# The ConvFFN of a diffusion block on one core: another order of the down-projection's K chunks, and four smaller moves in its schedule

## Chip, core and metric

One Trainium2 chip, one core of it. The metric is device time in microseconds (us) of one execution. The kernel before takes 1344.51 us (median of three runs, 1343.38 to 1346.95).

## What is computed

One layer of a hybrid backbone over 1024 latent tokens of width 1024: a mixing sub-layer (windowed attention beside Fourier mixing), then a gated MLP with a convolution over the tokens. The change lies in the second one:

```python
def conv_ffn(h, w_up, conv_w, conv_b, w_down):
    u, gate = jnp.split(h @ w_up, 2, axis=-1)                 # 1024 x 2816 each
    up = jnp.pad(u, ((0, 0), (1, 1), (0, 0)))
    u = up[:, :-2] * conv_w[0] + up[:, 1:-1] * conv_w[1] + up[:, 2:] * conv_w[2] + conv_b
    return (jax.nn.silu(u) * gate) @ w_down                   # 1024 x 1024
x = x + gt2 * rmsnorm(conv_ffn(h2, ...), g_post2)
```

All of it is float32.

## The kernel before

**Products.** Every large matrix product is cut into 2 x 2 blocks, and each block product is formed by a Winograd variant of Strassen's scheme with seven products, P1 to P7. It works on sums and differences of the operands' blocks: S1 to S4 of one operand (made per pair in `do_add`, L245), T1, T2, T3 and T4n of the other. A float32 operand is split into a high and a low float32r part (`split`, L79: ScalarE copies the high part, VectorE subtracts it to get the low one), and a product of two tiles takes three matmuls (`mm3`, L83).

**Items.** One of the seven products of one *pair* of blocks is an *item*. The list `items` (`wino_items`, L201) is the order of TensorE's work in the MLP: 17 items that are written out by hand (`START`, L1885), then seven per pair, P1 P2 P4 P3 P6 P5 P7, where P4 and P3 belong to the pair before. Items are counted here from 0. There are 22 *up pairs* (one per tile of 128 hidden columns, in the order 0, 11, 1, 12, ... 10, 21); up pair i, from the fourth on (i = 3), begins at item 19 + 7(i - 3), and an up item has 12 matmuls. The 16 *down pairs* begin at item 152: four chunks of K tiles, `CH` (L1663), each with four pairs of token tiles. HF is 11; the chunks are the K tiles 0-1, 2-4, 5-7 and 8-10, in this order, so a down item has 6 matmuls in chunk 0 and 9 in the others. The last item is 265.

**What sets the order.** The whole MLP is under a manual schedule: each engine and each DMA queue does its work in the order in which the program emits it, and all loads and stores are issued by the SyncE queue (SP). `run2` (L352) goes through the items. For item k it emits, in this order: hooks placed with `at(k, ...)`; `ahead(k)` (L328), which fetches and prepares operands of the next items; `flush(k)`, what earlier steps left due at k; the item's matmuls; and after P1, P6 and P7 a ScalarE copy of the accumulator X (tile `snP`). What comes due later is evacuation: the one of P7 reads accumulator Y at k + 2 (`add(gt[1], pst, sn)`, L1734, tile `gg`, or `yd` in the down stage), and P3 of the same pair, two items after that, accumulates into the same Y, so P3 waits for this read. In the same way P4 waits for the copy of X after P7.

**Up stage.** `ahead` loads the weights 11 items ahead, and makes S1 and S3 five items ahead; S2 and S4 follow. The engine for these four sums is `seng[0]`: VectorE until L2102 sets it to GpSimd, just before the general loop starts at item 14, and VectorE again from item 131 (L1909). After an up pair's last product comes the convolution: ScalarE scales, VectorE does two scalar_tensor_tensor (L1710, L1711), ScalarE the SiLU, VectorE two gate products. The result g is the down stage's first operand and goes to HBM (`g_d`, L1669). For P1, P2 and P4 it is always split first (`g_ready`, L1678: a ScalarE cast, a VectorE subtraction, tiles `gh` and `gl`, and three items later two stores). For the sums of P3, P5, P6 and P7 (`g_sums`, L1684, four operations on GpSimd up to f = 19 and on VectorE after), `split_early` (L1666) says whether they are split there as well, two stores each, or stored as they are:

```python
def split_early(c, p):
    return p in ("P1", "P2", "P4") or c in (0, len(CH) - 1)
```

**Weights of the down stage.** `d_diffs(r, i)` (L1757), for K tile r: at item i four loads of `w_down` into four buffers (`wB`, 4 buffers in all), at i + 4 to i + 7 one VectorE subtraction each, at i + 6 to i + 9 one store each. Before, i is 16 + 12 r. `d_prep` (L1789) loads a chunk's rows again (`wdB`, `wdT`), one per item, and splits them (`dB`, `dT`).

**Down stage.** `do_fetch` (L222) loads an item's g: six items ahead in two DMAs where it was split, nine items ahead in one where it was not. In chunk 0 the two parts share one tile (`b...`, L231), 128 x 256 each. In the last chunk `finish` (L1846) follows each complete half row of the output:

```python
rs = rstd_steps(ssd[:, i, :], f"d{i}")
return [(1, rs[0]), (2, lambda: [rs[1](), d_out(i, 0, rs[2]), d_out(i, 1, rs[2])] and None),
        (4, lambda: [d_store(i, h) for h in range(2)] and None)]
```

`rs[0]` is two small VectorE operations and ScalarE's square root (L142 to L144), `rs[1]` four small VectorE operations; before them stand the squares (`d_square`, ScalarE, L1824) and the gate (`d_gate`). What belongs to the last pair (token tiles 3 and 7) is written out after the loop (L2106 to L2130).

Of the kernel before, what the change touches and what calls it, by code (L numbers as in the profile page):

```python
# [16 lines left out]
P = 128  # L17
# [3 lines left out]
NT = S // P  # L21
# [3 lines left out]
NF = FF // P  # L25
# [15 lines left out]
def block_kernel(ctx: ExitStack, tc: tile.TileContext, t: dict, out: bass.AP, dbg: dict):  # L41
# [15 lines left out]
    def dscr(name, shape, dtype=F):  # L57
        return dram.tile(shape, dtype, tag=name, name=name)
# [78 lines left out]
    def rstd_steps(parts, name):  # L137

        v, sq, r, n1, r2 = (tiny(f"{n}{name}", 1, 16) for n in ("v", "sq", "r", "n1", "r2"))

        def one():
            add(v, parts[:, 0:1], parts[:, 1:2])  # L142
            nc.vector.tensor_scalar(out=v, in0=v, scalar1=1.0 / D, scalar2=EPS, op0=ALU.mult, op1=ALU.add)
            nc.scalar.activation(out=sq, in_=v, func=AF.Sqrt)  # L144

        def two():
            nc.vector.reciprocal(out=r, in_=sq)
            nc.vector.scalar_tensor_tensor(out=n1, in0=r, scalar=v, in1=r, op0=ALU.mult, op1=ALU.mult)
            nc.vector.tensor_scalar(out=n1, in0=n1, scalar1=-0.5, scalar2=1.5, op0=ALU.mult, op1=ALU.add)
            mul(r2, r, n1)  # L150

        return one, two, r2

    def transpose8(xn, psf, name):

# [55 lines left out]
    def wino(pairs, items, psf, hooks, slots=False, seng=None):  # L211
# [10 lines left out]
        def do_fetch(j, p):  # L222
            ld, _, nm, _, nk = pairs[j]
            parts = ld[p]
            w = nk * P
            if len(parts) == 1:
                st[j][STA[p]] = s(f"r{p}_{nm}")[:, :w]
                load(out=st[j][STA[p]], in_=parts[0])
                return
            if 2 * w <= 512:  # L230
                both = s(f"b{p}_{nm}", R)  # L231
                st[j][p] = both[:, :w], both[:, w:2 * w]
            else:
                st[j][p] = s(f"h{p}_{nm}", R)[:, :w], s(f"l{p}_{nm}", R)[:, :w]
            for x, src in zip(st[j][p], parts):
                load(out=fbits(x), in_=src)
# [1423 lines left out]


    HF = NF // 2
    CH = [(0, HF % 3)] + [(c, 3) for c in range(HF % 3, HF, 3)]  # L1663
    place = {c0 + k: (c, k) for c, (c0, nk) in enumerate(CH) for k in range(nk)}

    def split_early(c, p):  # L1666
        return p in ("P1", "P2", "P4") or c in (0, len(CH) - 1)

    g_d = {(c, p): [dscr(f"g_d{c}{p}{i}", [NT // 2, P, nk * P]) for i in range(2 if split_early(c, p) else 1)]  # L1669
           for c, (_, nk) in enumerate(CH) for p in STA}  # L1670
    kept = {}

    def g_store(f, p, *parts):
# [10 lines left out]
    def g_sums(f):  # L1684

        (a11, a21), (a12, a22) = kept[f - HF], kept[f]
        s1 = s(f"gs{f}")

        early = split_early(place[f % HF][0], "P5")

        def step(p, op, d, a, b):
            return lambda: (op(d, a, b, nc.gpsimd if f < NF - 2 else None), [(2, lambda: g_ready(f, p, d)) if early else (2, lambda: g_store(f, p, d))])[1]

        return [(0, step("P5", add, s1, a21, a22)), (0, step("P7", sub, a21, a11, a21)),
                (1, step("P6", sub, a11, s1, a11)), (3, step("P3", sub, a12, a12, a11))]
# [143 lines left out]

    def down_pair(c, m):  # L1840
        last = c == len(CH) - 1
        ld = {p: [d[m] for d in g_d[c, p]] for p in STA}

        half = set()

        def finish(i, n):  # L1846

            first = i not in half
            half.add(i)
            if not first and m == NT // 2 - 1:  # L1850
                return None

            def squares():
                d_square(i, n)
                d_gate(i, n)
                if first:
                    return None
                rs = rstd_steps(ssd[:, i, :], f"d{i}")
                return [(1, rs[0]), (2, lambda: [rs[1](), d_out(i, 0, rs[2]), d_out(i, 1, rs[2])] and None),
                        (4, lambda: [d_store(i, h) for h in range(2)] and None)]  # L1860
            return [(1, squares)]

        def ev(q, pst, sn):
# [31 lines left out]
    for c in range(len(CH)):  # L1895
        d_prep(c, NF + 4 * c - 1)
    for r in range(HF):
        d_diffs(r, 16 + 12 * r)

    def swap_misc():  # L1900
        miscF[0].release()
# [2 lines left out]
    def load_g2():  # L1904
        for h in range(2):
            G2.append(s(f"G2{h}"))
            load(out=G2[h], in_=gt_d[1, :, h * 512:(h + 1) * 512])

    at(pos[NF - 3, "P1"], lambda: seng.__setitem__(0, nc.vector))  # L1909
    at(pos[NF - 1, "P3"] + 6, swap_misc)  # L1910
    at(pos[NF + 12, "P1"], load_g2)
# [2 lines left out]
    with tc.manual_schedule():  # L1914
# [184 lines left out]
        for k in range(11, 14):  # L2099
            ahead(k)  # L2100
            evac(k)
        seng[0] = nc.gpsimd  # L2102
        M = len(items)
        run(14, M)

        i0, i1 = NT // 2 - 1, NT - 1  # L2106
        evac_last = due[M].pop()
        flush(M)
        d_square(i1, 0)
        d_gate(i1, 0)  # L2110
        rs1 = rstd_steps(ssd[:, i1, :], f"d{i1}")
        rs1[0]()
        rs1[1]()
        assert not evac_last()
        for k in (1, 2):
            flush(M + k)
        assert not due, sorted(due)
        d_square(i0, 1)
        d_out(i1, 1, rs1[2])
        d_store(i1, 1)  # L2120
        rs0 = rstd_steps(ssd[:, i0, :], f"d{i0}")
        rs0[0]()
        d_gate(i0, 1)
        rs0[1]()
        d_out(i0, 0, rs0[2])
        d_store(i0, 0)
        d_out(i0, 1, rs0[2])
        d_store(i0, 1)
        d_out(i1, 0, rs1[2])
        d_store(i1, 0)  # L2130
    miscD[0].release()
    hbl.release()
    hbp.release()
# [74 lines left out]
```

## Time and profile before

| | |
|---|---|
| median of 3 runs | 1344.51 us |
| the profiled execution's own time | 1345.93 us |
| span of its instructions | 1344.2 us |
| TensorE (PE) busy | 1275.7 us (95%), 5976 matmuls |
| VectorE (DVE) busy | 1037.4 us (77%) |
| ScalarE (ACT) busy | 691.6 us (51%) |
| GpSimd (POOL) busy | 272.0 us (20%) |
| mean granted TensorE clock | 0.988 |
| DMA | 254.57 MB, mean 189 GB/s |

Times in the rows are counted from the span's start. PEld is TensorE's weight load, SPq the SyncE queue that issues DMAs. "Idle before" is the time in which an engine stood still just ahead of an instruction, with the instruction that ended it. In the trace item 14 starts at 718.89, item 29 at 764.51, item 152 at 1102.00, item 180 at 1153.49 and the last item, 265, at 1332.27.

### The profile page before, as it was taken

Reading aid. Unit: us, or ns where it says so; the run is one execution under the profiler, and the core shown is the slowest. Engines: PE = TensorE matmul, PEld = TensorE weight load, DVE = VectorE, ACT = ScalarE, POOL = GpSimd, SP = SyncE. Lnnn points to the kernel's source line nnn. Section 1 sums busy time; section 2 is a strip of 40 time slices with the busy share of each in tenths; the row PEclk is TensorE's granted clock in tenths of the full one; section 3 lists DMA queues with packets and bytes.
Section 4 is the critical chain, followed back from the end, with each engine's and each line's share of the span. In section 5 each row is a group of like instructions: output and inputs, shape, how many; then the busy total and the mean of one; then the engine's idle time right before and its main releaser. Section 6 shows DMA issues by size and latency. Waiting matters only on the chain. (4 is left out here: it accounts for less than half of the span.)

```text
span 1344.2 us, 18657 instructions
## 1 busy us (share of the span) xinstructions
PE 1275.7 (95%) x5976; PEld 1024.8 (76%) x5976; DVE 1037.4 (77%) x1929; ACT 691.6 (51%) x1418; POOL 272.0 (20%) x216
## 2 busy tenths in 40 slices
PE   5889999999999999999999899999999998999996
PEld 3457877888878877778877788888888886688884
DVE  5687686976788896667879999778887987666767
ACT  6675345633567775344567454445444565444432
POOL 0000120200333333000004545534554100000000
PEclk9899999999999999999999899999999999999998
DMA  9986285513324344745213777565667789987974
GB/s 305 354 288 200 95 265 157 156 61 106 117 87 126 110 126 121 274 158 156 83 40 106 222 207 233 173 201 163 182 183 219 209 244 297 349 280 223 288 245 166
DMA packets 275606, 254.57 MB, mean 189 GB/s; under 512 B 17180, under 2 KB 214452, under 8 KB 275508
## 3 DMA queue, kind: packets, MB, share of 16 engines
q1 hardware_dynamic: 275508, 253.38, 60.8%
q8 instruction: 47, 0.77, 0.2%
q14 instruction: 51, 0.42, 0.1%
HBM read 179.65 MB, written 73.40 MB: 188 GB/s over the span
## 5 line engine op out<-in xcount | busy, mean ns | idle before, releaser
L68 DVE TENSOR_TENSOR lP_u<-A_u,hP_u 128x512 fp32r<-128x512 f32 x132 | 108.6, 829 | 30.0 <-ACT hP_u L303 28.4
L365 ACT COPY snP_u<-X_u 128x512 f32<-128x512 f32 x57 | 33.4, 586 | 134.8 <-PE X_u L87 134.0
L303 ACT CAST hP_u<-A_u 128x512 fp32r<-128x512 f32 x121 | 74.6, 619 | 0.1
L365 ACT COPY snP_d<-X_d 128x512 f32<-128x512 f32 x48 | 27.8, 584 | 88.2 <-PE X_d L87 83.8
L1305 POOL TENSOR_SCALAR p<-p,sm 128x640 f32<-128x640 f32 (+1 forms) x64 | 48.3, 774 | 91.7 <-PE pp L1310 40.1
L68 POOL TENSOR_TENSOR A_u<-A_u,A_u 128x512 f32<-128x512 f32 x35 | 57.9, 1655 | 24.7 <-DVE lP_u L68 11.9
L80 ACT CAST ph<-pp 128x512 fp32r<-128x512 f32 x76 | 44.3, 584 | 22.5 <-PE pp L1310 21.2
L68 DVE TENSOR_TENSOR pl<-pp,ph 128x512 fp32r<-128x512 f32 x76 | 51.6, 680 | 2.5 <-ACT ph L80 2.0
L1299 ACT ACTIVATE p<-p,nm 128x640 f32<-128x640 f32 (+1 forms) x64 | 51.4, 803 | 0.7 <-DVE nm L1292 0.7
L68 DVE TENSOR_TENSOR yd<-yd,snP_d 128x512 f32<-128x512 f32 x36 | 24.8, 690 | 32.6 <-ACT snP_d L365 32.6
L1285 DVE CUSTOM_DVE_ANT_0 p<-ss,mask 128x640 f32<-128x640 f32 (+1 forms) x64 | 49.8, 780 | 0.0
L1310 PE MATMUL pp<-ident,p 128*128 128x128 f32 x304 | 46.6, 274 | 2.8 <-POOL p L1305 1.5
L1310 PEld LDWEIGHTS pp<-ident,p 128*128 128x128 f32 x304 | 37.2, 140 | 11.7 <-POOL p L1305 2.9
L1710 DVE SCALAR_TENSOR_TENSOR tb<-u,vec,tb 128x1024 f32<-128x1024 f32 x22 | 41.9, 1904 | 3.6 <-ACT tb L1707 3.6
L68 POOL TENSOR_TENSOR A_u<-S_u,A_u 128x512 f32<-128x512 f32 x17 | 22.3, 1309 | 98.3 <-DVE lP_u L68 95.8
L68 DVE TENSOR_TENSOR lP_g<-A_g,hP_g 128x512 fp32r<-128x512 f32 x48 | 33.3, 699 | 9.8 <-ACT hP_g L80 9.8
L68 POOL TENSOR_TENSOR S_u<-A_u,A_u 128x512 f32<-128x512 f32 x17 | 34.3, 2020 | 30.4 <-PE X_u L86 30.4
L1281 PE MATMUL ss<-kst,qs 128*128 128x384 f32 (+1 forms) x128 | 36.5, 366 | 1.3 <-DVE mx L1285 0.8
L1711 DVE SCALAR_TENSOR_TENSOR tb<-u,vec,tb 128x1024 f32<-128x1024 f32 x22 | 36.4, 1656 | 0.9
L68 DVE TENSOR_TENSOR wB<-wB,wB 128x512 f32<-128x512 f32 x44 | 35.7, 810 | 0.0
L1321 PE MATMUL po<-pl,vst 128*128 128x512 f32 x76 | 31.3, 412 | 2.7 <-DVE pl L68 2.2
L1737 ACT COPY gf<-X_u 128x512 f32<-128x512 f32 x22 | 12.9, 586 | 38.4 <-PE X_u L87 37.8
(887 smaller groups left out, 4401.4 us busy)
## 6 DMA issues: line engine op xcount, KB each, us to landing
A_u<-in_w_up SPq DMA_DIRECT2D x88, 256.0 KB, 4.2
wB<-in_w_down SPq DMA_DIRECT2D x44, 256.0 KB, 4.7
wa<-in_w_mod SPq DMA_DIRECT2D x36, 256.0 KB, 5.3
wt_dT<-wB SPq DMA_DIRECT2D x33, 256.0 KB, 2.4
wdB<-in_w_down SPq DMA_DIRECT2D x33, 256.0 KB, 4.4
wdT<-wt_dT SPq DMA_DIRECT2D x33, 256.0 KB, 3.8
A_g<-in_w_in SPq DMA_DIRECT2D x32, 256.0 KB, 4.8
ws<-in_w_mod SPq DMA_DIRECT2D x30, 256.0 KB, 6.3
```

The costliest lines, as they stand in the source:

```text
L68: return (eng or nc.vector).tensor_tensor(out=out, in0=a, in1=b, op=op)
L80: copy(hi, src)
L303: copy(st[j]["half", p][0], st[j][STA[p]])
L365: copy(d["s" + p], d["X"])
L1281: nc.tensor.matmul(ssc[:, lo:512], self.qs[i][:, g * P:(g + 1) * P], kst[self.kv][:, self.k0 * P:self.k1 * P], start=i == 0, stop=i == 1)
L1285: nc.vector.tensor_tensor_reduce(out=p_, in0=ssc[:, lo:768], in1=self.mk, op0=ALU.add, op1=ALU.max, scale=1.0, scalar=-3.0e38, accum_out=s ...
L1299: nc.scalar.activation(out=self.pt[g], in_=self.pt[g], func=AF.Exp, scale=SCALE, bias=self.m[:, g:g + 1], accum_out=self.sm[:, g:g + 1])
L1305: nc.gpsimd.tensor_scalar(out=self.pt[g], in0=self.pt[g], scalar1=self.sm[:, g:g + 1], scalar2=1.0, op0=ALU.mult, op1=ALU.mult)
L1310: nc.tensor.transpose(pp[:, g * P:(g + 1) * P], self.pt[g][:, j * P:(j + 1) * P], ident)
L1321: nc.tensor.matmul(self.po, v_, self.parts[j][i], start=j == 0 and i == 0, stop=j == n - 1 and i == 1, skip_group_check=True)
L1710: nc.vector.scalar_tensor_tensor(out=tb, in0=u[:, 0:1024], scalar=cw[0], in1=tb, op0=ALU.mult, op1=ALU.add)
L1711: nc.vector.scalar_tensor_tensor(out=tb, in0=u[:, 2:1026], scalar=cw[2], in1=tb, op0=ALU.mult, op1=ALU.add)
```

## The change

Six things. (1) The chunks run in the order 0-1, 5-7, 8-10, 2-4: the chunk that is split early beside chunk 0 is now that of K tiles 2-4, not 8-10. (2) For chunk 0 the high and the low part lie side by side in one HBM tensor, and one DMA fetches both. (3) `d_diffs` starts at 32 + 10 r. (4) The pairs' sums stay on VectorE until item 32, and the four `g_sums` of f = 11 to 13 are on VectorE too. (5) `rstd_steps` gives the square root as a step of its own, and the last norms take their steps at items +1, +2, +3, +4 and +6 in place of +1, +2 and +4. (6) The code after the loop is put in a matching order; four output stores move into it.

```diff
 def rstd_steps(parts, name):
...
             nc.vector.tensor_scalar(out=v, in0=v, scalar1=1.0 / D, scalar2=EPS, op0=ALU.mult, op1=ALU.add)
+
+        def root():
             nc.scalar.activation(out=sq, in_=v, func=AF.Sqrt)
...
-        return one, two, r2
+        return one, two, r2, root
...
-            if 2 * w <= 512:
+            if len(parts) == 3:
                 both = s(f"b{p}_{nm}", R)
                 st[j][p] = both[:, :w], both[:, w:2 * w]
+                load(out=fbits(both[:, :2 * w]), in_=parts[2])
+                return
             else:
...
-    CH = [(0, HF % 3)] + [(c, 3) for c in range(HF % 3, HF, 3)]
+    CH = [(c, 3) for c in range(HF % 3, HF, 3)]
+    CH = [(0, HF % 3)] + CH[1:] + CH[:1]
...
-    g_d = {(c, p): [dscr(f"g_d{c}{p}{i}", [NT // 2, P, nk * P]) for i in range(2 if split_early(c, p) else 1)]
-           for c, (_, nk) in enumerate(CH) for p in STA}
+    g_d = {}
+    for c, (_, nk) in enumerate(CH):
+        for p in STA:
+            if nk < 3 and split_early(c, p):
+                d = dscr(f"g_d{c}{p}", [NT // 2, P, 2 * nk * P])
+                g_d[c, p] = [d[:, :, i * nk * P:(i + 1) * nk * P] for i in range(2)]
+                g_both[c, p] = d
+            else:
+                g_d[c, p] = [dscr(f"g_d{c}{p}{i}", [NT // 2, P, nk * P]) for i in range(2 if split_early(c, p) else 1)]
...
-            return lambda: (op(d, a, b, nc.gpsimd if f < NF - 2 else None), [(2, lambda: g_ready(f, p, d)) if early else (2, lambda: g_store(f, p, d))])[1]
+            return lambda: (op(d, a, b, nc.gpsimd if HF + 2 < f < NF - 2 else None), [(2, lambda: g_ready(f, p, d)) if early else (2, lambda: g_store(f, p, d))])[1]
...
-        ld = {p: [d[m] for d in g_d[c, p]] for p in STA}
+        ld = {p: [d[m] for d in g_d[c, p]] + ([g_both[c, p][m]] if (c, p) in g_both else []) for p in STA}
...
-                return [(1, rs[0]), (2, lambda: [rs[1](), d_out(i, 0, rs[2]), d_out(i, 1, rs[2])] and None),
-                        (4, lambda: [d_store(i, h) for h in range(2)] and None)]
+                return [(1, rs[0]), (2, rs[3]), (3, lambda: [rs[1](), d_out(i, 0, rs[2])] and None),
+                        (4, lambda: d_out(i, 1, rs[2])), (6, lambda: [d_store(i, h) for h in range(2)] and None)]
...
-        d_diffs(r, 16 + 12 * r)
+        d_diffs(r, 32 + 10 * r)
...
+    at(32, lambda: seng.__setitem__(0, nc.gpsimd))
     at(pos[NF - 3, "P1"], lambda: seng.__setitem__(0, nc.vector))
...
-        seng[0] = nc.gpsimd
         M = len(items)
         run(14, M)
...
-        flush(M)
+        due[M], rest = [], due[M]
+        for fn in rest:
+            fn()
         d_square(i1, 0)
+        rs1 = rstd_steps(ssd[:, i1, :], f"d{i1}")
+        rs0 = rstd_steps(ssd[:, i0, :], f"d{i0}")
+        rs1[0]()
+        rs1[3]()
         d_gate(i1, 0)
-        rs1 = rstd_steps(ssd[:, i1, :], f"d{i1}")
-        rs1[0]()
         rs1[1]()
         assert not evac_last()
-        for k in (1, 2):
-            flush(M + k)
-        assert not due, sorted(due)
         d_square(i0, 1)
         d_out(i1, 1, rs1[2])
         d_store(i1, 1)
-        rs0 = rstd_steps(ssd[:, i0, :], f"d{i0}")
         rs0[0]()
+        rs0[3]()
         d_gate(i0, 1)
+        for k in range(7):
+            flush(M + k)
+        assert not due, sorted(due)
         rs0[1]()
-        d_out(i0, 0, rs0[2])
-        d_store(i0, 0)
-        d_out(i0, 1, rs0[2])
-        d_store(i0, 1)
-        d_out(i1, 0, rs1[2])
-        d_store(i1, 0)
+        for i, n, r in ((i0, 1, rs0), (i0, 0, rs0), (i1, 0, rs1)):
+            d_out(i, n, r[2])
+            d_store(i, n)
```

## Rows read from the trace of the kernel before

**Rows 1.** Stretches: us; busy of PE, PEld, DVE, ACT, POOL; PEclk, DMA share, GB/s

```profile
740.00:760.00 20.00, 20.00 (x90) 16.57 (x89) 19.82 (x19) 8.86 (x15) 11.55 (x7) 1.00 0.71 208
760.00:780.00 20.00, 16.18 (x60) 12.83 (x59) 18.56 (x21) 9.53 (x17) 8.93 (x6) 0.83 0.70 197
1100.00:1120.00 20.00, 18.80 (x82) 14.90 (x80) 18.60 (x27) 14.76 (x25) 0.00 (x0) 1.00 0.93 266
1120.00:1140.00 20.00, 16.98 (x73) 13.81 (x74) 14.54 (x24) 11.16 (x21) 0.00 (x0) 0.98 1.01 307
1140.00:1160.00 20.00, 16.79 (x62) 11.58 (x62) 8.26 (x14) 7.10 (x13) 0.00 (x0) 0.94 1.02 336
1300.00:1320.00 20.00, 19.26 (x84) 15.30 (x83) 15.52 (x34) 6.01 (x17) 0.00 (x0) 1.00 0.91 296
```

**Rows 2.** TensorE's waits over the whole span: us in total, times, longest

```profile
PE Y_u L85 <- DVE gg L68: 4.0, 2, 3.8
...
PE Z_d L85 <- DMA bP_d<-g_d0P: 2.8, 1, 2.8
...
PE Y_d L85 <- DVE yd L68: 2.0, 3, 1.3
```

**Rows 3.** Order of time, VectorE, GpSimd, TensorE, 739 to 765: start, us, instruction

```profile
739.20 0.68 DVE L68 TENSOR_TENSOR lP_u<-S_u,hP_u 128x512 fp32r<-128x512 f32 x1
739.80 1.27 DVE L1710 SCALAR_TENSOR_TENSOR tb<-u,vec,tb 128x1024 f32<-128x1024 f32 x1
...
746.34 1.62 POOL L68 TENSOR_TENSOR A_u<-S_u,A_u 128x512 f32<-128x512 f32 x1 [11.22 <-DVE lP_u L68]
...
746.72 1.78 DVE L68 TENSOR_TENSOR gg<-gg,tb 128x512 f32<-128x512 f32 x1
...
763.17 0.68 DVE L68 TENSOR_TENSOR gg<-gg,tb 128x512 f32<-128x512 f32 x1
763.78 0.68 DVE L68 TENSOR_TENSOR gg<-Y_u,snP_u 128x512 f32<-128x512 f32 x1
...
764.51 0.80 PE L85 MATMUL Y_u<-B22a,hP_u 128*128 128x512 f32 x1 [3.81 <-DVE gg L68]
```

**Rows 4.** Stretches around the general loop's start and after it, columns as above

```profile
714.00:764.30 50.30, 45.33 (x198) 36.58 (x196) 49.92 (x62) 29.91 (x55) 30.87 (x15) 0.99 0.51 152
764.30:800.00 35.70, 35.49 (x144) 29.17 (x145) 31.85 (x37) 17.01 (x29) 18.42 (x12) 0.91 0.80 233
800.00:920.00 120.00, 120.00 (x532) 99.37 (x531) 100.25 (x121) 57.49 (x95) 53.62 (x36) 1.00 0.65 194
```

**Rows 5.** The stretch of chunk 0's stall, columns as above

```profile
1108.00:1152.00 44.00, 36.81 (x151) 28.29 (x150) 28.80 (x45) 21.65 (x38) 0.00 (x0) 0.96 1.00 301
```

**Rows 6.** DMA issues by tile: count, ns min/median/max, first and last start

```profile
L236 SPq DMA_DIRECT2D bP_d<-g_d0P x56: 319/430/1462, 1079.3 to 1155.8; - x56
...
L1676 SPq DMA_DIRECT2D g_d3P<-ghP x11: 371/383/642, 1101.5 to 1142.1; - x11
```

**Rows 7.** Order of time, the SyncE queue around 1136

```profile
1134.50 1.93 SPq L1796 DMA_DIRECT2D wdT<-wt_dT  x1
1136.53 0.86 SPq L236 DMA_DIRECT2D bP_d<-g_d0P  x2
```

**Rows 8.** The last items in order of time; DMA to landing of the output stores

```profile
1327.97 0.15 DVE L68 TENSOR_TENSOR vd<-ssd 128x1 f32<-128x1 f32 x1
...
1328.34 0.20 ACT L144 ACTIVATE sqd<-vd 128x1 f32<-128x1 f32 x1 [3.78 <-DVE vd L143]
...
1329.07 0.50 PE L85 MATMUL X_d<-dT4n,hP_d 128*128 128x512 f32 x1 [3.38 <-ACT snP_d L365]
...
1331.53 0.69 DVE L68 TENSOR_TENSOR yd<-yd,Y_d 128x512 f32<-128x512 f32 x1
...
1337.14 4.22 SPq L1833 DMA_DIRECT2D out<-yd  x4
...
DMA to landing us min/median/max: 2.0/2.1/6.2
```

More of the change, by code (lines that the diff above doesn't have):

```diff
@@ L1662, in block_kernel @@
     HF = NF // 2
-    CH = [(0, HF % 3)] + [(c, 3) for c in range(HF % 3, HF, 3)]
+    CH = [(c, 3) for c in range(HF % 3, HF, 3)]
+    CH = [(0, HF % 3)] + CH[1:] + CH[:1]
     place = {c0 + k: (c, k) for c, (c0, nk) in enumerate(CH) for k in range(nk)}
+    g_both = {}
     def split_early(c, p):
         return p in ("P1", "P2", "P4") or c in (0, len(CH) - 1)
-    g_d = {(c, p): [dscr(f"g_d{c}{p}{i}", [NT // 2, P, nk * P]) for i in range(2 if split_early(c, p) else 1)]
-           for c, (_, nk) in enumerate(CH) for p in STA}
+    g_d = {}
[7 more added lines that the diff above has]
+                g_d[c, p] = [dscr(f"g_d{c}{p}{i}", [NT // 2, P, nk * P]) for i in range(2 if split_early(c, p) else 1)]
     kept = {}
```

## The prediction, made before the changed kernel had run

> **What bounds the kernel now.** TensorE. I read the stretches of 20 us first: undisturbed, TensorE starts 90 matmuls in 20 us [rows 1], one per 0.222 us, so a missing one is 0.222 us lost, whether it waited or ran at a low clock. An up item (12 matmuls) is then 2.67 us, a chunk 0 item (6) 1.33 us. Nearly all of the MLP runs at 90; only a few stretches don't, and only these can give time back.
>
> - 760 to 780 has 60: 30 x 0.222 = **6.7 us**. The waits name it: Y_u on VectorE's gg, 3.8 us at most [rows 2]; the order of time shows the place, item 29, with TensorE idle for 3.81 us until VectorE has read Y [rows 3]. The rest is clock: the mean granted clock of the stretch is 0.83 [rows 1], so after the idle time it ran for a while at the lower of the two levels, 1.2 and 2.4 GHz; 6.7 - 3.8 = 2.9 us.
> - 1100 to 1160 has 82, 73 and 62: 8, 17 and 28 missing, 1.8 + 3.8 + 6.2 = **11.8 us**. Here the waits are for the DMAs of chunk 0's g (tile bP_d, longest 2.8 us) and, 2.0 us in three, for VectorE's yd [rows 2]; the DMA engines' busy share is 0.93, then 1.01 and 1.02 [rows 1].
> - 1300 to 1320 has 84: **1.3 us**. After that comes the tail, where the matmuls of item 264 wait 3.38 us for a ScalarE copy [rows 8].
>
> So the ceiling is about 20 us plus some of the tail.
>
> **The change part by part.**
>
> *VectorE ahead of item 29 (the sums, and d_diffs later).* From 714 to 764.3 VectorE is busy for 49.92 of 50.30 us, and GpSimd does 15 operations beside it [rows 4]. All 15 move to VectorE (eleven of the pairs' sums, four of f = 11). Alone, a two-input VectorE operation is followed by the next after 0.60 us and a scalar_tensor_tensor takes 1.27 [rows 3]. From 746.72 to 763.17 VectorE does nine of the first kind and two of the second without a pause; alone they are 9 x 0.60 + 2 x 1.3 = 8.0 us, here 16.45. The first of them takes 1.78 us where the same operation takes 0.68 at 763.17 [rows 3]. Eight GpSimd operations run in that time, the first at 746.34 after 11.22 us of idleness, in which the short ones stand [rows 3]: each costs VectorE some 8.4 / 8 = 1.05 us, by blocking it. Done on VectorE it costs 0.60. The removal of 15 is then worth between 8.4 us (only those eight block) and 15.8, against 9.0 added. The first set of d_diffs has its four subtractions at items 20 to 23, before item 29, and they go to items 36 to 39: 4 x 0.60 = 2.4 us more. VectorE reaches the read of Y earlier by 8.4 + 2.4 - 9.0 = 1.8 us at least and 9.2 at most; it has to be 3.8 us. The blocking in the eight is the nearest row for the other seven, so I take the upper half: the stall goes, **6.7 us**; the lower bound is 1.8.
>
> What then waits behind VectorE's new work: a sum waits for weights loaded six items before it and for a free buffer, and the low parts and the reads of Y stand behind it. Until now it was GpSimd that waited there. VectorE is at that place later than GpSimd was, so I cost this at nothing; bound 0 to 1 us.
>
> The Trainium skill speaks against this part: its page Perfetto Trace Analysis, section Optimizing Scalar/DVE Operations, holds that where VectorE is saturated it may make sense to offload to GpSimd, while it warns that between these two it might not help. By the first half alone, the sum of this part would be the 9.0 us of new VectorE work less 2.4, a loss; it comes back below the slower rival. The rows with and without GpSimd beside VectorE bear out the warning.
>
> *The other chunk split early.* K tiles 8 to 10 no longer get P3, P5, P6 and P7 split in the up stage. For f = 19, 20 and 21 that drops four casts, four subtractions and four of eight stores each, and the four that are left are issued three items earlier; f = 19's lie before 1100, where nothing stalls. The stores of this chunk's high parts from 1101.5 to 1142.1 are 11 [rows 6], and each has one of a low part behind it: 22, of which 14 are left. The eight are 8 x 256 KB = 2.1 MB, and the DMA engines are full from 1108 to 1152, at 301 GB/s [rows 5]: 2.1 MB / 301 GB/s = **7.0 us** of transfer less in the stretch that DMA bounds. TensorE loses 45 x 0.222 = 10.0 us from 1120 to 1160 [rows 1], of which 1.3 is VectorE's yd [rows 2], so 8.7 are there to be had. The lower bound is 3.5 (the four stores of f = 20 lie before 1113, and if the DMA engines catch up there, only f = 21's count), the upper 8.7. I take 7.0. VectorE's three subtractions of f = 20 that stand before its last read of Y_u, 1.8 us, free the 0.2 us wait there [rows 2]: 0.3 with the clock. The wait for yd follows a chain over ScalarE that the change leaves alone: nothing.
>
> *One DMA for chunk 0's two parts.* 56 issues [rows 6] become 28. The bytes stay, so I cost the transfer at nothing. On the SyncE queue it is 28 x 0.43 = 12.0 us less [rows 6]. That counts: two fetches take 0.86 us of the queue [rows 7], and a weight load of some 0.45 goes with each item, 1.31 us of the item's 1.33 with no store among them; a store in front makes the queue late (one load issue there took 1.93 us [rows 7]). Afterwards it is 0.43 + 0.45. With the queue no longer full, the 7.0 us are DMA's to give; I add nothing.
>
> *What this costs in the up stage.* f = 13 to 15 are split early instead: 12 casts, 12 subtractions, 12 more stores; in items 32 to 90 there is one more set of d_diffs (36, 46, ... 86: six, where 32, 44, ... 80 were five), 4 subtractions; f = 13's four sums come to VectorE. 20 VectorE operations from 800 to 920, where it is busy 100.25 of 120 us with 121 instructions, 0.83 each [rows 4]: 16.6 us into 19.75 idle. Cover: that idle time; if each takes the blocked 1.70 it is 34 us, and TensorE loses up to 34 - 19.75 - 8 x 1.05 (the relief of eight sums) = 6 us. I take 0. ScalarE is busy under half, DMA 0.65 [rows 4]: hidden. d_diffs' loads now come one item after the last set's store, not three: the queue may wait for the store to land (2.1 us, at most 6.2, for stores of this size [rows 8]) less an item of 2.67, at most 3.5 us. Behind it stand weight loads that are issued 11 items, 29 us, ahead: nothing.
>
> *The last norms.* Item 264 waits because the ScalarE copy after item 263 stands behind a square root which waits 3.78 us for VectorE [rows 8]. With the root one step later the copy goes first. But then VectorE is late next: item 265 needs yd's read of Y, which starts at 1331.53 [rows 8]. What stands before that read loses one output operation, which now comes after it (0.7), the round trip from 1327.97 to the root and back (0.6 [rows 8]), and the wait for the pair's other root, which now stands behind the squares (0.4, an estimate at two thirds of that trip): 1.7 us; with the 1.3 us of 1300 to 1320, whose waits are of the same kind (two of yd's three, 2.0 - 1.3 = 0.7 [rows 2], and the items after them), 3.0. Against it: four earlier output stores now stand behind the first of the last four, whose issues take 4.22 us in all and which land 2.1 us after [rows 8], 6.3 us. Eight land in 2.1 + 7 x 0.87 = 8.2 us if each goes at the 301 GB/s of rows 5; the trace has no eight in a row. So the end comes 0 to 1.9 us later; I take half, 1.0. **2.0 us**; bounds 0.5 and 4.5 (all of 3.38 and 1.3).
>
> **Sum.** 6.7 + 7.0 + 0.3 + 2.0 = 16.0 us. The profiled execution took 1345.93 us (span 1344.2), so 1329.9; the median, 1344.51, is 1.4 lower: **1328.5 us**. A measurement of this kernel can tell about 0.3%, 4 us, from no change.
>
> **Rivals.**
> 1. *DMA stays the bound of chunk 0.* For it: most of what is moved stays (14 stores, the weight loads), and the share is 1.01 and more until 1160 [rows 1]. Then 3.5 instead of 7.0: 1332. Against: the stretch is short of transfer time by just about what is dropped. 20%.
> 2. *Item 29 still waits for VectorE*, since only the eight late GpSimd operations block: 1.8 instead of 6.7: 1333.4. Against: the blocking is a pattern of every pair of operations that meet. 13%.
> 3. *Slower: VectorE becomes the bound of the up stage.* Its stretched operations stay stretched without GpSimd's work. Place: items 14 to 90. Price: 9.0 - 2.4 - 0.4 (idle) = 6.2 us at item 29; the twenty operations at 1.70, 34 - 19.75 = 14 us, from 800 to 920; 2.9 us of low clock, as after the stall of now: 23 lost. Item 29's 6.7 are not won, so 16.0 - 6.7 = 9.3 are left of the sum, and it comes out 14 us slower: 1358. It decides once the losses pass 9.3 us, so with 6.2 at item 29 from (3.1 + 19.75) / 20 = 1.14 us for each of the twenty. Against it: 0.68 beside 1.78 [rows 3]. 6%. This is also what the first half of the rule in the Trainium skill's Perfetto Trace Analysis would lead to.
> 4. *Several terms fail together* and under 4 us are left: 6%.
>
> The forecast has 55%. That the chunks are not split as said can't be: `split_early` goes by the chunk's place.
>
> **Range.** Rivals 1 and 2 together give 16.0 - 3.5 - 4.9 = 7.6 us, 1337; the upper bounds give 6.7 + 8.7 + 0.3 + 4.5 and the yd wait, 1.3: 21.5 us, 1323. I say 1322 to 1337. Faster by over 0.3%: 55 + 20 + 13 = 88%; within: 6%; slower: 6%.
>
> **What would show it.** Right: 760 to 780 near 90 matmuls with VectorE's operations before it at 0.68; 14 stores of the g of K tiles 8 to 10 in place of 22, 28 fetches of bP_d, and 1 to 3 us missing in the 60 us from item 152 on; the copy after item 263 directly at its end. Wrong: a wait of Y_u for gg anywhere from item 29 to 90; the waits for bP_d at half their size or more; a last store over 2 us after its fellows.

## The result, and the profile after

The changed kernel takes **1326.73 us** (median of four runs, 1325.21 to 1328.54) against 1344.36 for the kernel before beside it: ratio 0.9866, 95% interval 0.9848 to 0.9885. The forecast was 1328.5, within 1322 to 1337.

The page of its profiled execution (1326.39 us of its own time), busy time by engine:

```profile
span 1324.6 us, 18599 instructions
...
PE 1266.2 (96%) x5976; PEld 1021.8 (77%) x5976; DVE 1046.2 (79%) x1954; ACT 691.2 (52%) x1418; POOL 231.3 (17%) x191
```

To see where the time went, both spans are cut at the starts of the same items: 14, 16, 32, 90, 152, 171, 190, 250 and 264. In every execution such a stretch holds the same work, so a difference in its length (second column) is time lost or won there. Columns are as in [rows 1]. The kernel before:

```profile
725.17:775.60 50.43, 46.62 (x194) 38.04 (x192) 48.64 (x52) 25.46 (x39) 28.09 (x17) 0.93 0.60 172
775.60:933.36 157.76, 157.76 (x698) 130.68 (x696) 129.86 (x152) 75.41 (x124) 72.16 (x49) 1.00 0.67 199
...
1102.00:1132.61 30.61, 29.16 (x127) 23.50 (x126) 28.22 (x44) 19.99 (x35) 0.00 (x0) 1.00 1.00 296
1132.61:1173.22 40.61, 34.62 (x140) 26.03 (x138) 21.84 (x37) 18.66 (x35) 0.00 (x0) 0.96 1.02 336
...
1295.62:1329.07 33.45, 29.33 (x127) 23.31 (x126) 26.07 (x66) 9.93 (x28) 0.00 (x0) 1.00 0.69 229
1329.07:1344.16 15.09, 6.19 (x18) 4.14 (x18) 10.81 (x27) 2.58 (x8) 0.00 (x0) 0.77 0.32 119
```

The changed kernel, the same stretches:

```profile
723.89:767.41 43.52, 43.52 (x193) 36.04 (x192) 41.74 (x60) 25.30 (x39) 2.19 (x2) 1.00 0.48 133
767.41:926.82 159.41, 158.35 (x697) 130.48 (x696) 150.95 (x176) 80.69 (x136) 64.92 (x41) 1.00 0.76 226
...
1095.46:1125.60 30.14, 28.87 (x128) 23.57 (x127) 23.95 (x37) 17.17 (x29) 0.00 (x0) 1.00 0.88 283
1125.60:1156.88 31.28, 31.28 (x140) 25.90 (x139) 21.65 (x37) 18.38 (x35) 0.00 (x0) 1.00 1.04 372
...
1279.28:1308.67 29.39, 28.72 (x127) 23.46 (x125) 23.38 (x56) 10.34 (x28) 0.00 (x0) 1.00 0.66 222
1308.67:1324.61 15.94, 4.67 (x18) 3.23 (x18) 11.44 (x30) 2.52 (x9) 0.00 (x0) 0.82 0.36 132
```

Where PE's busy time equals the length, nothing is lost: items 32 to 90 before, 58 x 12 = 696 matmuls in 157.76 us, 0.2267 each. The stretches that aren't shown are equal in both, but for the one before item 14, 1.3 us shorter in this execution. The change does not touch it, and in the executions of the same program text below it ends between 716.3 and 718.8. The rest, in us won: 6.91 at items 16 to 32 (the stall at item 29 is gone), -1.65 at 32 to 90, 0.47 at 152 to 171, **9.33** at 171 to 190 (chunk 0's stall is gone), 4.06 at 250 to 264, -0.85 in the end: 18.3 us, where the medians differ by 17.6.

VectorE's read of Y that item 29 waits for, the same instruction as at 763.78 in [rows 3]:

```profile
756.04 0.68 DVE L68 TENSOR_TENSOR gg<-Y_u,snP_u 128x512 f32<-128x512 f32 x1
```

It ends 39.12 us after item 14's start; before, it ended 45.57 us after it.

TensorE's waits in the changed kernel, as in [rows 2]:

```profile
PE Y_d L85 <- DVE yd L68: 2.4, 2, 1.3
...
PE Y_u L85 <- DVE gg L68: 1.1, 2, 0.6
```

bP_d is no longer among them. The wait for gg, which was one of 3.8 us at item 29, is now two new ones of about 0.6. The order of time shows one, ahead of item 71 (VectorE, then TensorE):

```profile
862.34 1.78 DVE L68 TENSOR_TENSOR glP<-gs,ghP 128x512 fp32r<-128x512 f32 x1
864.05 1.78 DVE L68 TENSOR_TENSOR glP<-gg,ghP 128x512 fp32r<-128x512 f32 x1
865.75 2.32 DVE L1724 SCALAR_TENSOR_TENSOR tb<-u,vec,tb 128x1024 f32<-128x1024 f32 x1
...
873.52 0.69 DVE L68 TENSOR_TENSOR gg<-Y_u,snP_u 128x512 f32<-128x512 f32 x1
...
874.26 0.50 PE L85 MATMUL Y_u<-B22a,hP_u 128*128 128x512 f32 x1 [0.61 <-DVE gg L68]
```

The two subtractions that make the low parts of f = 14 (new here) stand in VectorE's queue ahead of the convolution and the read of Y, each at its long duration. At the end, the copy after item 263 now comes first and the matmul of item 264 waits 0.68 us for it, not 3.38 [rows 8]:

```profile
1308.67 0.50 PE L85 MATMUL X_d<-dT4n,hP_d 128*128 128x512 f32 x1 [0.68 <-ACT snP_d L369]
```

The stores of the outputs, from DMA to landing:

```profile
DMA to landing us min/median/max: 2.0/2.9/4.2
```

In [rows 8] the median was 2.1: eight stand behind one another now, where it was four.

### The profile page after: what moved, and what is told of

Read it like the earlier page. It is cut to its first block, busy times and chain, and to the rows that moved or that the text cites. A ratio compares the mean times of both kernels' runs of the same rounds, so it can differ in the third digit from the quotient of the medians.

```text
span 1324.6 us, 18599 instructions
## 1 busy us (share of the span) xinstructions
PE 1266.2 (96%) x5976; PEld 1021.8 (77%) x5976; DVE 1046.2 (79%) x1954; ACT 691.2 (52%) x1418; POOL 231.3 (17%) x191
## 4 chain that ended last, share of the span: by engine, by line
PE 68%; DVE 15%; DMA 8%; ACT 4%; issue 3%; SPq 2%; POOL 1%; DVEq 0%; ACTq 0%; POOLq 0%
PE X_u L87 5%; PE X_u L85 5%; PE X_u L86 5%; PE X_d L87 3%; PE X_d L85 3%; PE X_d L86 3%; PE Y_u L85 3%; PE Y_u L87 3%; PE Y_u L86 3%; DVE p L1289 2%; PE X_g L85 2%; PE X_g L86 2%; PE X_g L87 2%; DMA ws<-in_w_mod 2%; DVE pl L68 2%
## 5 line engine op out<-in xcount | busy, mean ns | idle before, releaser
L68 POOL TENSOR_TENSOR A_u<-A_u,A_u 128x512 f32<-128x512 f32 x28 | 47.9, 1711 | 13.9 <-DVE lP_u L68 6.1
L68 POOL TENSOR_TENSOR S_u<-A_u,A_u 128x512 f32<-128x512 f32 x14 | 23.7, 1696 | 88.3 <-DMA g_d0P<-ghP 81.8
L68 POOL TENSOR_TENSOR A_u<-S_u,A_u 128x512 f32<-128x512 f32 x14 | 18.7, 1338 | 104.1 <-DVE lP_u L68 101.7
L1728 ACT ACTIVATE tb<-tb 128x1024 f32<-128x1024 f32 x22 | 23.4, 1063 | 16.6 <-DVE tb L1725 16.6
```

The costliest lines, as they stand in the source:

```text
L68: return (eng or nc.vector).tensor_tensor(out=out, in0=a, in1=b, op=op)
```

## Experiments

Each starts from the changed kernel. "Loss" is the length of a stretch beyond the undisturbed one: 43.52 us for items 16 to 32, 157.76 for 32 to 90, 31.28 for 171 to 190. The stretches are read from one execution of each kernel. From item 14 on, where an edit leaves a stretch alone, its length repeats within 0.3 us (items 90 to 152: 168.64 in every one of the fourteen traces), while the time of the unaltered changed kernel goes from 1325.21 to 1328.54. So small parts are read from the stretches.

### Chunk 0: which part took the stall away

**e1_old_order:**

```diff
-    CH = [(0, HF % 3)] + CH[1:] + CH[:1]
+    CH = [(0, HF % 3)] + CH
```

> The changed kernel with the chunks in the order of before (0-1, 2-4, 5-7, 8-10), so that K tiles 8 to 10 are split early again and their eight stores are back late in the up stage; the one fetch of both parts stays. Theory (the sum of the prediction): the stores were worth 7.0 us of the stall in chunk 0; with the early splits of f = 13 to 15 gone, the two new waits of Y_u for gg (1.1 us, and about 1.7 us with the slow start behind them) go too: 1326.7 + 7.0 - 1.7 = 1332.0 us, waits for bP_d of 4 us and more in the trace. Rival 1 (the single fetch took the stall away by itself): no wait for bP_d over 0.5 us, 1325.0 us. Rival 2 (the single fetch is worth nothing): the whole 9.3 us comes back, 1334.3 us.

**e2_two_fetches:**

```diff
-                load(out=fbits(both[:, :2 * w]), in_=parts[2])
-                return
+                parts = parts[:2]
```

> The changed kernel, but chunk 0's high and low part are fetched by two DMAs of 128 KB in place of one of 256 KB (28 issues more; the layout in HBM and the stores stay). Theory (as predicted: the single fetch adds nothing to what the dropped stores give): no wait for bP_d, 1326.7 us within 1.3. Rival 1 (the single fetch took away the part of the stall that the stores did not, 9.3 - 7.0): waits for bP_d of about 2 us, 1329.0 us. Rival 2 (the single fetch took it all, by its larger pieces or by the SyncE queue): 1336.0 us, and a rate of the DMA engines in the 40 us from item 152 + 12 us on at 307 GB/s as in the kernel before, not 351 as in the changed one.

**e5_both_undone** is e1 and e2 together.

> The changed kernel with the old order of the chunks and with two fetches of 128 KB for chunk 0: both parts of the change around chunk 0 undone together. Undone alone they brought 2.75 us (order) and 1.74 us (fetches) of loss back in items 172 to 189, of the 9.3 there before. Theory (the two replace one another: either alone gives most of it): more than the sum of the two, about 9 us of loss, 1326.7 + 9.3 + 0.5 - 1.7 = 1334.8 us, the 1.7 being the waits for gg at items 71 and 85, which the old order does not have. Rival (the parts add up, and the rest of the old stall had other causes, such as the later start of the down stage): 2.75 + 1.74 = 4.5 us of loss, 1330 us.

Items 171 to 190, one row each, e1 first:

```profile
1125.67:1159.70 34.03, 32.17 (x139) 25.53 (x138) 21.77 (x37) 18.26 (x35) 0.00 (x0) 1.00 1.06 372
```

e2:

```profile
1125.60:1158.62 33.02, 32.42 (x139) 25.45 (x138) 21.87 (x37) 18.37 (x35) 0.00 (x0) 1.00 0.99 335
```

e5:

```profile
1124.22:1165.24 41.02, 33.92 (x140) 24.81 (x139) 22.04 (x37) 18.56 (x35) 0.00 (x0) 1.00 1.01 325
```

Losses: 2.75, 1.74 and **9.74**. Medians: 1328.04, 1328.81 and 1333.83 us. In e1 all three values miss: the order alone brings back neither nothing, nor 7.0, nor all of it. In e2 the time is the first rival's (2 us beside the stores), but its waits of about 2 us for bP_d are not there: the loss lies at items 179 to 182, in waits of 0.3 us at most, some of them for the next chunk's g. The reason for both is that the parts do not add up, they *replace* one another, and e5's loss is what its theory said. With two fetches the order of chunks is worth 9.74 - 1.74 = 8.0 us, with one fetch 2.75; the single fetch is worth 6.99 in the old order and 1.74 in the new. e5 brings back the old stall, so the two parts are its whole cause. (In e1 and e5 the waits at items 71 and 85 are gone: f = 13 to 15 are not split early.) In e5 it is not bP_d alone that comes late. One of TensorE's waits is for a weight, whose load goes through the same queue:

```profile
PE X_d L85 <- ACT dT L1814: 1.8, 1, 1.8
```

**Why the single fetch gives.** By the size of its pieces or by the SyncE queue's time:

**e6_half_rows** (old order):

```diff
-                load(out=fbits(both[:, :2 * w]), in_=parts[2])
+                for r in range(0, P, P // 2):
+                    load(out=fbits(both[r:r + P // 2, :2 * w]), in_=parts[2][r:r + P // 2])
```

> Old order of the chunks, and chunk 0's two parts fetched by two DMAs again, but each takes both parts for 64 of the 128 partitions: 56 issues on the SyncE queue as in the kernel before, and pieces of 2 KB as in the single fetch, not of 1 KB. Beside the old order with a single fetch (2.75 us lost in items 172 to 189) and with two fetches by parts. Theory A (the single fetch gives by the size of its pieces, which the DMA engines move faster): 2.75 us lost, about 1328 us. Theory B (it gives by the 28 issues that the SyncE queue is spared): the loss of two fetches by parts, about 9 us, 1334.8 us. Between the two, both count.

**e11_extra_issues** (old order):

```diff
                 load(out=fbits(both[:, :2 * w]), in_=parts[2])
+                load(out=dmy[0][:1, 2 * len(dmy):2 * len(dmy) + 2], in_=parts[2][:1, :2])
+                dmy.append(nm)
...
+    dmy = [small.tile([P, 60], F, name="dmy")]
```

> Old order of the chunks with the single fetch (2.75 us lost in items 172 to 189), and behind each of the 28 fetches a DMA of 8 bytes, one piece, into a tile that nobody reads: 56 issues on the SyncE queue as with two fetches, and neither bytes nor pieces that count. Theory B (the two fetches cost by their issues on the SyncE queue, 28 x 0.43 = 12 us): a loss near the 9.7 us of both undone, about 1334 us. Theory A (they cost by their pieces of 1 KB, which the DMA engines move slower): 2.75 us, 1328 us as with the old order alone. Between: by the share of each.

e6, the stretch, and its fetches' issues (ns min/median/max):

```profile
1125.37:1170.36 44.99, 35.58 (x138) 27.30 (x139) 21.35 (x36) 16.84 (x32) 0.00 (x0) 0.92 1.04 314
```

```profile
L236 SPq DMA_DIRECT2D bP_d<-g_d0P x56: 444/588/1051, 1069.8 to 1150.7; - x56
```

e11, the same:

```profile
1123.08:1160.66 37.58, 33.01 (x139) 25.20 (x138) 22.05 (x37) 18.47 (x35) 0.00 (x0) 1.00 1.00 332
```

```profile
L237 SPq DMA_DIRECT2D dmy<-g_d0P x28: 240/290/442, 1069.5 to 1143.1; - x28
```

e6 loses 13.71 us in the stretch (1342.18 us), more than two fetches by parts and far from both theories' numbers: pieces of 2 KB are no help when there are 56 issues. It is not a clean test of the size, as each of its fetches fills half of the partitions: its issue is longer, 0.59 us and not 0.43, and it lands 4.2 us after it, not 3.8 as in e5. e11 loses 6.30 (1330.24 us), between its theories: 3.55 more than e1, for 28 DMAs that move 224 bytes. Set against the time that each adds to the SyncE queue over the single fetch's 28 x 0.43 = 12.0 us: e11 28 x 0.29 = 8.1 us for 3.55 of loss, e5 12.0 for 6.99, e6 56 x 0.588 - 12.0 = 20.9 for 10.96; 0.44, 0.58 and 0.52 us lost (beyond e1's 2.75) for each us of the queue. So the places on the queue, theory B, carry about half of it or more; at e11's price the 12.0 us of queue would be 5.3 of the 6.99, and what the other 1.7 are (longer issues, pieces of 1 KB) stays open.

The queue itself shows it. SyncE in e5, in a stretch with stores:

```profile
1124.68 1.10 SPq L1689 DMA_DIRECT2D g_d3P<-glP  x1
1125.88 1.16 SPq L1809 DMA_DIRECT2D wdT<-wt_dT  x1
1127.13 1.44 SPq L239 DMA_DIRECT2D bP_d<-g_d0P  x2
```

In the changed kernel:

```profile
1124.29 0.43 SPq L1810 DMA_DIRECT2D wdT<-wt_dT  x1
1124.92 0.32 SPq L235 DMA_DIRECT2D bP_d<-g_d0P  x1
1125.58 0.32 SPq L1810 DMA_DIRECT2D wdT<-wt_dT  x1
```

There one issue follows the other and takes up to 1.2 us; here an issue takes 0.32 to 0.43 and the queue pauses between two. Over the whole stretch from item 158's start to item 180's, in which the fetches for these items are issued, 66 issues take 32.5 of 39.4 us in e5, 40 issues 17.7 of 31.5 in the changed kernel.

**Why the dropped stores give. e13_store_issues** (new order, two fetches):

```diff
+    tiny_d = dscr("tiny_d", [HF, 16])
...
+        extra = lambda p: [(5, lambda: store(out=tiny_d[f % HF:f % HF + 1, 2 * int(p[1]):2 * int(p[1]) + 2], in_=vec[:1, :2]) and None)] if f > 18 else []
...
-            return lambda: (op(d, a, b, nc.gpsimd if HF + 2 < f < NF - 2 else None), [(2, lambda: g_ready(f, p, d)) if early else (2, lambda: g_store(f, p, d))])[1]
+            return lambda: (op(d, a, b, nc.gpsimd if HF + 2 < f < NF - 2 else None), [(2, lambda: g_ready(f, p, d)) if early else (2, lambda: g_store(f, p, d))] + extra(p))[1]
```

> The changed kernel with two fetches (as e2: 1.74 us lost in items 172 to 189), and for f = 19, 20 and 21 twelve stores of 8 bytes where the old order has the stores of the low parts of P3, P5, P6 and P7: their places on the SyncE queue without their 256 KB each, their casts and their subtractions. Theory (as predicted: the eight dropped stores of the stretch gave by their transfer): 28 small DMAs cost 3.55 us in e11, 0.13 us each, so eight to twelve cost 1.0 to 1.5: 2.7 to 3.2 us lost, 1328.5 us. Rival (they gave by their places on the queue): the 9.7 us of both undone come back, 1335 us.

```profile
1124.80:1159.11 34.31, 32.92 (x140) 25.21 (x138) 21.75 (x37) 18.27 (x35) 0.00 (x0) 1.00 0.98 336
```

```profile
L1704 SPq DMA_DIRECT2D tiny_d<-vec x12: 246/292/326, 1055.1 to 1129.8; - x12
```

3.03 us lost, 1.29 more than e2 (1328.43 us): the theory. But the place of a small store is a shorter one, 0.29 us of the queue against 0.38 for a real one [rows 6]. So of the 8.0 us that the stores are worth beside two fetches, at least 1.3 are their places on the queue. At most 6.7 are their transfer, together with the casts and subtractions that go with them and the three items by which the stores that are left come earlier; these were not tried apart.

### VectorE ahead of item 29, and in the up stage

**e3_sums_gpsimd:**

```diff
-            return lambda: (op(d, a, b, nc.gpsimd if HF + 2 < f < NF - 2 else None), [(2, lambda: g_ready(f, p, d)) if early else (2, lambda: g_store(f, p, d))])[1]
+            return lambda: (op(d, a, b, nc.gpsimd if f < NF - 2 else None), [(2, lambda: g_ready(f, p, d)) if early else (2, lambda: g_store(f, p, d))])[1]
-    at(32, lambda: seng.__setitem__(0, nc.gpsimd))
+        seng[0] = nc.gpsimd
         M = len(items)
```

> The changed kernel with the pairs' sums from item 14 on and the g_sums of f = 11 to 13 back on GpSimd; the differences of w_down stay at 32 + 10 r. Theory: from item 14's start to the end of the read of Y that item 29 waits for it is 39.1 us in the changed kernel and 45.6 in the one before; of the 6.5 us between, 2.4 are the four subtractions that are moved and 4.1 the sums. TensorE wants the read done at 41.65, so without the sums it waits 39.1 + 4.1 - 41.65 = 1.5 us, with the slow start behind it about 2.5: 1329.2 us. Rival 1 (the subtractions did it all): no wait at item 29, 1326.7 us or less. Rival 2 (only the sums did it): 3.8 us of wait and 6.7 lost, 1333.4 us.

**e4_diffs_early:**

```diff
-        d_diffs(r, 32 + 10 * r)
+        d_diffs(r, 16 + 12 * r)
```

> The changed kernel with the differences of w_down back at 16 + 12 r. Theory: the four subtractions, 4 x 0.60 = 2.4 us, take nearly all of the 2.53 us by which the read of Y is ahead of item 29: no wait there or one below 0.5 us, and one set fewer lies between items 32 and 90, so at items 71 and 85 the waits of Y_u for gg (1.1 us together) shrink: 1326.2 us, between 1325 and 1327.5. Rival 1 (the moved subtractions are the main part of it): a wait of 1.5 us or more at item 29, 1329 us and above. Rival 2 (the sums on VectorE are what gives and the sets' places count for nothing anywhere): the two waits at 71 and 85 unchanged, 1326.7 us.

**e8_all_vector:**

```diff
-            return lambda: (op(d, a, b, nc.gpsimd if HF + 2 < f < NF - 2 else None), [(2, lambda: g_ready(f, p, d)) if early else (2, lambda: g_store(f, p, d))])[1]
+            return lambda: (op(d, a, b, None), [(2, lambda: g_ready(f, p, d)) if early else (2, lambda: g_store(f, p, d))])[1]
-    at(32, lambda: seng.__setitem__(0, nc.gpsimd))
-    at(pos[NF - 3, "P1"], lambda: seng.__setitem__(0, nc.vector))
```

> The changed kernel with all of the pairs' sums and all g_sums on VectorE; GpSimd does nothing in the up stage after the start. Theory (a GpSimd operation beside VectorE costs it more than the operation itself): from 800 to 920 the changed kernel's VectorE is busy for 112.1 us, of which 26.2 are over the durations that its operations have undisturbed, with 34 GpSimd operations beside it; 112.1 - 26.2 + 34 x 0.60 = 106.3 us, so the two waits for gg at items 71 and 85 go: 1326.7 - 1.7 = 1325.0 us, VectorE's operations at 0.68 throughout. Rival (VectorE is the busier engine and work moved to it is added to it): 112.1 + 34 x 0.60 = 132.5 us for a stretch of 120, so TensorE loses 12.5 us there, 1339 us or more; to items 90 to 130, too, the waits for gg come.

Items 16 to 32 and 32 to 90, e3:

```profile
723.52:769.07 45.55, 43.82 (x194) 35.97 (x193) 44.20 (x46) 25.48 (x39) 25.04 (x15) 1.00 0.45 125
769.07:930.64 161.57, 158.70 (x698) 130.36 (x696) 156.74 (x167) 80.61 (x136) 81.96 (x51) 1.00 0.75 224
```

e4:

```profile
725.07:768.59 43.52, 43.52 (x193) 36.04 (x192) 42.76 (x63) 25.43 (x39) 1.39 (x1) 1.00 0.61 175
768.59:927.47 158.88, 158.25 (x697) 130.40 (x696) 150.46 (x176) 81.72 (x136) 63.87 (x42) 1.00 0.76 223
```

e8:

```profile
724.78:768.30 43.52, 43.52 (x193) 36.04 (x192) 41.76 (x62) 25.30 (x39) 0.00 (x0) 1.00 0.48 133
768.30:926.06 157.76, 157.76 (x697) 130.63 (x696) 145.82 (x217) 81.58 (x136) 0.00 (x0) 1.00 0.79 232
```

e3 (1330.7 us, forecast 1329.2) loses 2.03 us up to item 32, near the theory's 2.5, and 3.81 after it, 2.16 more than the changed kernel, which no theory had. What differs there in the program are the g_sums of f = 11 to 13, back on GpSimd; how they make for the later waits was not followed. e4 (1326.7 us) loses nothing at item 29 and 1.12 after it, as the theory said. So the sums alone end the stall, the moved differences alone end 6.91 - 2.03 = 4.9 us of it, and the changed kernel does both where the first would do. Here, too, the parts replace each other.

e8 is the plainest. Its time, 1325.75 us, can't be told from the changed kernel's, but its stretch can: it loses nothing, where the changed kernel loses 1.65. From item 32 to 90, 41 operations go from GpSimd to VectorE, and VectorE's busy time *falls* from 150.95 to 145.82 us. Without them VectorE would have 145.82 - 41 x 0.60 = 121.2 us; beside GpSimd it had 150.95, so each of the 41 cost it 29.7 / 41 = 0.73 us, against 0.60 to do it [rows 3]. From e3 to the changed kernel at items 16 to 32 it is the same: 13 operations leave GpSimd, VectorE has 14 more and is busy for 41.74 in place of 44.20, so each had cost it (44.20 - 41.74 + 14 x 0.60) / 13 = 0.84. The spread of one operation shows that some of them are stretched beside GpSimd (ns min/median/max), first in the changed kernel, then in e8:

```profile
L68 DVE TENSOR_TENSOR lP_u<-A_u,hP_u x132: 675/684/1784, 634.5 to 1096.3; 128x512 fp32r<-128x512 f32 x132
```

```profile
L68 DVE TENSOR_TENSOR lP_u<-A_u,hP_u x132: 677/684/694, 635.4 to 1095.5; 128x512 fp32r<-128x512 f32 x132
```

The Trainium skill's page Perfetto Trace Analysis, section Optimizing Scalar/DVE Operations, suggests moving work off a saturated VectorE, to GpSimd too, and adds that between these two it might not help. The measurement decides here for the warning, and goes further: on these operations, two inputs of 128x512 float32, it costs more than it frees.

### The last norms, and a better version

**e7_norms_undone** puts the steps back:

```diff
-                return [(1, rs[0]), (2, rs[3]), (3, lambda: [rs[1](), d_out(i, 0, rs[2])] and None),
-                        (4, lambda: d_out(i, 1, rs[2])), (6, lambda: [d_store(i, h) for h in range(2)] and None)]
+                return [(1, lambda: [rs[0](), rs[3]()] and None), (2, lambda: [rs[1](), d_out(i, 0, rs[2]), d_out(i, 1, rs[2])] and None),
+                        (4, lambda: [d_store(i, h) for h in range(2)] and None)]
```

with the code after the loop as before.

> The changed kernel with the steps of the last norms and the code after the loop as before (square root at + 1, both output halves at + 2, stores at + 4; the four earlier stores ahead of the last four). Theory: the losses come back where they were, 1.35 us at items 253 and 260, 4.7 in place of 2.3 us at items 264 and 265, 0.67 us of the last item; and the end after the last item is 1.2 us shorter: 1326.7 + 1.35 + 2.4 + 0.7 - 1.2 = 1330.0 us. Rival 1 (2.0 us as predicted): 1328.7 us. Rival 2 (the steps only shift the waits to the end): 1326.7 us within 0.5.

Items 250 to 264 and the end:

```profile
1279.34:1312.80 33.46, 29.33 (x128) 23.31 (x126) 26.08 (x66) 9.93 (x28) 0.00 (x0) 0.99 0.72 230
1312.80:1328.30 15.50, 5.73 (x18) 4.32 (x18) 10.73 (x27) 2.58 (x8) 0.00 (x0) 0.72 0.31 116
```

1330.12 us. 4.07 us come back up to item 264, and the end is 0.44 shorter: the steps are worth 3.6 us. The time is the theory's; the end was to be 1.2 us shorter, and why it is not stays open.

**e10_best** has e8's edits, the flush of the four earlier stores moved ahead of the last pair's code, and

```diff
-            return [(1, conv), (2, silu), (3, gate)] + rest
+            z = int(f == NF - 1)
+            return [(1, conv), (2, silu), (3 + z, gate)] + [(n + z, fn) for n, fn in rest]
...
-        if len(yd) < 3:
+        if len(yd) < 4:
...
-    at(pos[NF - 1, "P3"] + 6, swap_misc)
+    at(pos[NF - 1, "P3"] + 7, swap_misc)
```

> All sums on VectorE (as in e8), and two more moves. The four earlier output stores are issued ahead of the last four. The two gate products of the last up pair come one item later, behind the read of Y_d that item 162 waits for (the change of pools is an item later too). Theory: the last store lands 2.06 us after its issue again, not 2.93, so the end comes 0.9 us earlier; the read of Y_d at 1112.48 is brought forward by two operations, 1.2 us, which leaves 0.3 of the 1.56 us lost at items 162 and 163. With the 1.7 us of items 71 and 85: 1326.7 - 1.7 - 0.9 - 1.2 = 1322.9 us. Rival (the ends of the waits move elsewhere, the gate products delay the last g, and the stores wait for one another in any order): 1325.7 us as in e8.

**e12_after_again** is the changed kernel unaltered, beside e10.

> The changed kernel unaltered, for comparison on the same chip: 1326.7 us, 0.9866 of the kernel before, and the same losses by item as in its first profile: 1.66 us at items 71, 72, 85 and 86, 1.56 at 162 and 163, 2.3 at 264 and 265, none from 172 to 189.

e10, items 32 to 90, 152 to 171 and the end:

```profile
766.58:924.34 157.76, 157.76 (x698) 130.63 (x696) 145.85 (x217) 81.55 (x136) 0.00 (x0) 1.00 0.78 232
...
1092.98:1121.88 28.90, 28.85 (x128) 23.57 (x126) 24.00 (x37) 17.19 (x29) 0.00 (x0) 1.00 0.91 282
...
1305.11:1320.18 15.07, 4.67 (x18) 3.22 (x18) 11.44 (x30) 2.52 (x9) 0.00 (x0) 0.79 0.37 139
```

Against the changed kernel's rows: 1.65, 1.24 and 0.87 us less, each as its theory said, and 0.16 more at items 171 to 190. **e10 takes 1322.07 us** (1321.96 to 1323.13; ratio 0.9843 to the kernel before, 0.9830 to 0.9857), e12 1325.97 (1325.46 to 1326.79; 0.9870, 0.9856 to 0.9883): it beats both kernels. e12's losses are those of the first profile, within 0.2 us a stretch.

## Why the prediction was right

- **The count, 0.222 us for a matmul:** undisturbed it is 0.2267, 2% more. That moves no term by more than 0.3 us.
- **Item 29, 6.7 us:** measured 6.91, of which the low clock was part, as read (0.93 over items 16 to 32 before, 1.00 now). VectorE is done with the read of Y 6.45 us sooner after item 14's start, in the upper half of 1.8 to 9.2, as chosen. The step that it rested on, that all the GpSimd operations stretch VectorE's and not just the eight late ones, is borne out by e3 and e8; its price of 1.05 us was that of a crowded stretch, and 0.73 to 0.84 is the mean.
- **Dropped stores, 7.0 us of transfer:** beside two fetches they are worth 8.0, at most 6.7 of it transfer (e13). That is near 7.0. But beside the single fetch, which the changed kernel has, the order is worth only 2.75 (e1). So the prediction's split, 7.0 for the stores and nothing for the fetch, is just one way to share a joint gain.
- **The single fetch, "I add nothing":** this term was mis-sized. It is 1.74 us on top of the stores (e2), and 6.99 by itself in the old order. Order and fetch together were put at 7.0 and gave 9.33. The 12.0 us of queue were counted in the step, but the DMA engines at a share of 1.01 were taken for the bound that makes them worthless. The same items ran at 325 GB/s in e5 and 372 in the changed kernel, both at a share of 1.0 and more: a full share was no fixed rate.
- **Item 155, 0.3 us:** 0.47, and it comes back with the old order: items 152 to 171 last 30.59 us in e1 and 30.61 in e5.
- **Last norms, 2.0 us:** 4.06 - 0.85 = 3.2, within its bounds. What was won up to the last matmul was put at 3.0 and is 4.43; the later end was put at 1.0 and is 1.22, of which e10, with the four stores ahead again, takes 0.87 back.
- **Up stage, 0:** 1.65 us lost at items 71 and 85. A wait of Y_u for gg between items 29 and 90 was one of the prediction's own signs of being wrong. The step that failed set 16.6 us of work against 19.75 of idle time over 120 us. The work did fit, with VectorE busy 112.1 of the 120 us. But its queue was late where the low parts of an early split met GpSimd's operations, ahead of the read of Y of two pairs: without the splits (e1, e5) and without GpSimd's operations (e8) nothing is lost there. The bound of 6 held.
- **The wait for yd at item 162, nothing:** unchanged in length, but not for the reason given, a chain over ScalarE. Two gate products stood ahead of the read of Y on VectorE:

```profile
1111.27 0.69 DVE L68 TENSOR_TENSOR gf<-gf,tb 128x512 f32<-128x512 f32 x1
1111.88 0.69 DVE L68 TENSOR_TENSOR gg<-gg,tb 128x512 f32<-128x512 f32 x1
1112.48 0.68 DVE L68 TENSOR_TENSOR yd<-Y_d,snP_d 128x512 f32<-128x512 f32 x1
```

e10 moved them behind it and won 1.24 us.
- **Rivals.** The first (DMA stays the bound) and the second fell with the rows above. The third, VectorE as the bound of the up stage, was refuted by e8: all the work on VectorE loses nothing.

Three terms were off: chunk 0 (2.3 us too little), the last norms (1.2 too little) and the up stage (1.65 too much). The signs differ, so the sum, 16.0 us for a measured 18.3, is 2.3 off where the three together are 5.2 off; that much is luck.

## What to carry to other kernels

Before work goes to GpSimd, or stays there, take the time by which VectorE's operations exceed their undisturbed length and divide it by the number of GpSimd operations beside them. If that is more than the operation costs on VectorE, try taking it back, however busy VectorE is; here it held for sums of two 128x512 float32 tiles, and other shapes were not tried. A DMA has two prices, its bytes and its place on the issuing queue; where a queue is full, joining two transfers that always go together can be worth as much as moving fewer bytes. And parts of a change that attack one stall replace each other: undo them singly and together before giving each its share.

## What the runs showed of the hardware that was not expected

- **No more than eight DMAs were under way.** In the kernel before, from item 14 to 265, 511 issues have a recorded landing of the DMA eight places ahead in the SyncE queue. None starts before that landing (the earliest 0.02 us after it, 80 within 0.25 us); of the DMA seven places ahead, 98 start before its landing. The changed kernel has the same (484 issues, none, 77). The program gives its DMAs eight semaphores in turn, so the bound may be the program's. It can be part of why a DMA of 8 bytes is not free, as it holds one of eight places until it lands; that was not tried by itself. In e5, where issues take 32.5 of the 39.4 us from item 158 to 180, the pauses that end within 0.25 us of such a landing sum to 3.0 us. There the issues themselves take most of the queue's time; why single ones take 1.1 us stays open.
- **The issue's length was not fixed.** 0.32 us at the shortest, for fetches of 128 KB and of 256 KB alike, whose medians are 0.43 in both; 0.59 is the median of a fetch of 128 KB by half the partitions.
- **The clock did not fall for every stall.** e5 lost 9.74 us at items 171 to 190 with a granted clock of 1.00, the kernel before 9.33 with 0.96; e3's waits for gg, 1.7 us at most, left it at 1.00, where the one wait of 3.8 in the kernel before had 0.93 over the same items.
